# A two-layer hybrid attention block: mixer parts recorded in a common time, attention steps regrouped, early feed-forward chunks cut from six to four

## The chip, the cores and the metric

The kernel is one program on one NeuronCore of a Trainium2 chip. The metric is the device time of one execution in microseconds. Inputs lie in device memory when the time starts; the host only reorders weights. Engine names are those of the profile: PE (TensorE matmuls), PEld (its weight loads), DVE (VectorE), ACT (ScalarE), POOL (GpSimd), SP (SyncE, which issues the DMAs).

## The reference

One sequence of 512 tokens with 1024 features passes through two layers. Each layer has a first feed-forward block, a mixer and a second feed-forward block, with a layer norm after each (`ALPHA * x` is added first; the feed-forward outputs are halved). All values are 32-bit floats.

```python
D_MODEL, SEQ, DEPTH, D_FF = 1024, 512, 2, 2816
N_GROUPS, HEADS, HEAD_DIM, D_GROUP, Q_BLOCK = 4, 4, 64, 256, 128

def swiglu(x, w1, w3, w2):
    return (jax.nn.silu(x @ w1) * (x @ w3)) @ w2

def hybrid_mixer(x, w_in, ...):
    h = split_columns(x @ w_in)
    y_a = mla_mixer(...)              # latent attention, softmax
    y_b = nsa_mixer(...)              # compressed + selected + window attention, gated
    y_c = dsa_mixer(...)              # an indexer picks the top keys, then softmax attention
    y_d = stick_breaking_mixer(...)
    y = jnp.concatenate([y_a, y_b, y_c, y_d], -1).reshape(B, S, N_GROUPS, D_GROUP)
    y = rms_norm(y, group_norm_g.reshape(N_GROUPS, D_GROUP)).reshape(B, S, D_MIX)
    return y @ w_out

def masked_softmax(s, mask):
    s = jnp.where(mask, s, NEG_INF)
    e = jnp.where(mask, jnp.exp(s - jnp.max(s, -1, keepdims=True)), 0.0)
    return e / jnp.maximum(jnp.sum(e, -1, keepdims=True), 1e-30)
```

Each mixer group has four heads of width 64, and works through four blocks of 128 queries. In block b only the first (b + 1) * 128 keys count.

## The kernel before

**Numbers.** A 32-bit product of the large matrices is made of three passes: each factor is split in a rounded part (`hi`) and the rest (`lo`), and `mm3` issues hi*hi, hi*lo and lo*hi. A weight unit (`wunit`) is a DMA of 128 x 1024 values into a `raw` buffer, a rounding copy into `whi` and a DVE subtraction into `wlo`. The input x of each stage lies transposed in `xhi` and `xlo`; the residual stream lies in `z`.

**Feed-forward.** The hidden width is cut in 22 chunks of 128. A chunk has an up part (w1 and w3), and its down part (w2) follows when a group of chunks is there: for each of the four token blocks and each half of the output one PSUM tile collects the group, and DVE adds it to `z`. There are two kinds of up part. `up` is plain: 8 x 3 matmuls for each of w1 and w3, with 512 tokens, or 256 where half of the tokens are treated. `up_pair` takes both weights together over combinations of token halves and weight halves (a Strassen-like scheme): 7 products of 4 x 3 matmuls with 256 columns, after `token_sums` has formed the sums and differences of x on DVE. In layer 0 the first block takes its first two chunks plainly and all others by `up_pair`.

**The second feed-forward block in two halves.** `EARLY` chunks are taken for tokens 0 to 255 inside the mixer (`ffn_half(..., 0)`, called the filler) and for tokens 256 to 511 after it (`ffn_half(..., 1)`), both with plain `up`; `REST` chunks follow by `up_pair`.

**The mixer.** It consists of Python generators: `index_proj`, `sb_proj`, `mla_proj`, `nsa_proj`, `dsa_proj` project; `index_scores` and `choose` score keys and pick 128 of them by 16 steps of `max` and `match_replace` on DVE for each of three blocks (the tiles named `acc`); `sb_attend`, `mla_attend`, `nsa_attend`, `dsa_attend` are the groups. The three softmax groups go through `attend`: for each head scores into a PSUM tile `ps`, a maximum on DVE, an exponential on ACT that also sums, transposes on PE, a copy, and the product with the values into `po`. `group_out` then normalizes a group's block, multiplies it with `w_out` and adds to `z`; `dsa_attend` ends a block with its layer norm. `proj_rope` projects, copies out of PSUM (`evac`) and rotates (`roped`).

**What sets the order.** Every operation is recorded (so nearly all carry line 400, the call in `emit`; copies carry 388, scaled copies 396). `Plan.schedule` then plays the program with its own cost table and gives every engine the ready operation that was recorded first, if its buffers can be had; a buffer out of turn is given only while more than `reserve` of its kind are free. An operation for "scalar/vector" goes to whichever is free, except that DVE leaves it when ACT will be free within `BEHIND` ns. The recording order is thus the priority. It is written by `weave`, which steps a main generator and others at a rate, for instance `weave(mla_attend((1, 0, 3, 2)), (npj, 0.3), (chooser, 1.3))`, and `drain`.

Of the kernel before, what the change touches and what calls it, by code (L numbers as in the profile page):

```python
# [14 lines left out]
OP = mybir.AluOpType  # L15
# [11 lines left out]
EARLY = (3, 3)  # L27
REST = (6, 5, 5)
# [4 lines left out]
WA = 468  # L33
# [110 lines left out]
class Plan:  # L144
# [4 lines left out]
    BEHIND = 700  # L149
# [93 lines left out]
    def schedule(self):  # L243
# [42 lines left out]
        while left:  # L286
            progress = True
            while progress:
                progress = False
                for e in engines:  # L290
# [4 lines left out]
                    while h:  # L295
                        x = heapq.heappop(h)[2]
                        x.queued.discard(e)
                        if x.start is None and eligible(x):
                            if e == "vector" and "scalar" in x.costs and free_at["scalar"] < now + self.BEHIND:
# [177 lines left out]
def block_kernel(ctx, tc, ins, out, dbg=None):  # L477
# [13 lines left out]
    t_lo = pl.tag(sb, "wlo", 6, [1024], F32R, reserve=2)  # L491
# [7 lines left out]
    singles = {n: pl.tag(sb, n, 1, [w]) for n, w in (("mv", 4 * 256), ("acc23", 7 * P))}  # L499
# [345 lines left out]
    def roped(zs, spans):  # L845

        sw, o = tmp(), ht()
        rope = rope_now[0]
        for r0, rn, tb in spans:
# [10 lines left out]
    def proj_rope(w, spans, scale=None):  # L860
        return roped(evac(projT(w), tmp(), scale), spans)
# [11 lines left out]
    def attend(b, qk, v, mask, o, rs):  # L873

        n = (b + 1) * P
        sums = small(4)
        for h in range(4):
            s = psc()
            for i, (q, k) in enumerate(qk(h)):
                PE.matmul(s[:, :n], q, k, start=(i == 0), stop=False)  # L880
            if mask is None:
                PE.matmul(s[:, n - P:n], identb, maskd, start=False, stop=True)
            else:
                PE.matmul(s[:, :n], identb, mask, start=False, stop=True)
            m = small(1)
            V.tensor_reduce(m, s[:, :n], axis=AX, op=OP.max, negate=True)
            e = tmp()
            A.activation(e[:, :n], s[:, :n], AF.Exp, bias=m, accum_out=sums[:, h:h + 1])
            pt = transposed(None, e, n)
            et = tmp()  # L890
            AV.tensor_copy(et[:, :n], pt[:, :n])
            for j in range(b + 1):
                PE.matmul(o[:, h * 64:(h + 1) * 64], et[:, j * P:(j + 1) * P], v(h, j), start=(j == 0), stop=(j == b))
            yield
        V.tensor_scalar(rs, sums, 1e-30, None, op0=OP.max)
        V.reciprocal(rs, rs)

    def heads(t):
        return t.split(4)

# [6 lines left out]
    def group_out(b, y, gcol, wo):  # L907
# [4 lines left out]
        r = rsqrt(ss, 1, 1e-6)  # L912
        pt = ptr()
        for c in range(2):
            PE.transpose(pt[:, c * P:(c + 1) * P], y[:, c * P:(c + 1) * P], ident)
        yh = pl.buf(t_yh, [2, P], F32R)
        yl = pl.buf(t_yl, [2, P], F32R)
        for c in range(2):
            cs = slice(c * P, (c + 1) * P)
            AV.scaled(yh[:, c, :], pt[:, cs], gcol[:, c:c + 1])  # L920
            V.scalar_tensor_tensor(yl[:, c, :], pt[:, cs], gcol[:, c:c + 1], yh[:, c, :].bitcast(F32),
                                   op0=OP.mult, op1=OP.subtract)
        for n in range(2):
            ns = slice(n * 512, (n + 1) * 512)
            p = pm()
            for c in range(2):
                mm3(p, (yh[:, c, :], yl[:, c, :]), (wo[c][0][:, ns], wo[c][1][:, ns]), c == 0, c == 1)
            V.scalar_tensor_tensor(z[:, b, ns], p, r, z[:, b, ns], op0=OP.mult, op1=OP.add)


    def weave(main, *others):

        due = [0.0] * len(others)
        for _ in main:
            for i, (gen, rate) in enumerate(others):
                due[i] += rate
                while due[i] >= 1:
                    due[i] -= 1
                    next(gen, None)
# [5 lines left out]
    def mixer(l, filler):  # L945
# [7 lines left out]
        def wout(g):  # L953
            return [wunit(wo[(2 * g + c) * P:(2 * g + c + 1) * P, :]) for c in range(2)]
# [36 lines left out]
        V_SLC, V_WIN, V_DSA, V_SB, V_G, V_IW = 0, 64, 128, 192, 448, 460  # L991
# [80 lines left out]
        def sb_attend(blocks):  # L1072
            w_sb = wout(3)
            for b in blocks:
# [26 lines left out]
                group_out(b, y, gc[:, 6:8], w_sb)  # L1101
# [5 lines left out]
        mv = single("mv", [NB, 256])  # L1107

        def mla_proj():
# [40 lines left out]
            for c in (2, 0, 1):  # L1150
# [3 lines left out]
                if c == 2:  # L1154
                    qr = roped(evac(p, tmp(), M_SCALE), FULL_I)
# [12 lines left out]
            for h in range(4):  # L1168
                move(mk[h][64:96, :], krT[0:32, :])
            for b in range(NB):  # L1170
                p = pm()
                PE.matmul(p[:, :256], ckT[:, b * P:(b + 1) * P], uk[:, 256:512], start=True, stop=True)
                AV.tensor_copy(mv[:, b, :], p[:, :256])
            yield

        def mla_attend(blocks):
            w_mla = wout(0)
            for b in blocks:
# [4 lines left out]
                                  lambda h, j: mv[:, j, h * 64:(h + 1) * 64], None, o, rs)  # L1183
                y = ytile()
                V.tensor_tensor(heads(y), heads(o[:, :256]), bc(rs), op=OP.mult)
                dump(f"y_a{l}_{b}", y)
                group_out(b, y, gc[:, 0:2], w_mla)
# [98 lines left out]
        def nsa_attend(blocks):  # L1286
            w_nsa = wout(1)
            kslc, kwin, ec = nk
            for b in blocks:
# [7 lines left out]
                for g, (kk, v0) in enumerate(((kslc, V_SLC), (kwin, V_WIN))):  # L1297
# [20 lines left out]
        def dsa_attend(blocks, gb):  # L1318
            w_dsa = wout(2)
            for b in blocks:  # L1320
# [5 lines left out]
                                  lambda h, j: vt[:, j, V_DSA:V_DSA + 64], None if b == 0 else bias[b][:, :n], o, rs)  # L1326
                y = ytile()
                V.tensor_tensor(heads(y), heads(o[:, :256]), bc(rs), op=OP.mult)
                dump(f"y_c{l}_{b}", y)
                group_out(b, y, gc[:, 4:6], w_dsa)  # L1330
# [9 lines left out]
        drain(index_proj())  # L1340
        drain(sb_proj())
        isc = index_scores((3, 2, 1))
        mp = mla_proj()
        weave(sb_attend(range(NB)), (isc, 1.5), (mp, 0.3), (chooser, 0))
        drain(isc)
        drain(mp)
        pl.ln = False
        npj, dpj = nsa_proj(), dsa_proj()
        weave(mla_attend((1, 0, 3, 2)), (npj, 0.3), (chooser, 1.3))
        drain(npj)  # L1350
        weave(nsa_attend((0, 1)), (dpj, 0.15), (chooser, 0.8))
        drain(dpj)
        gb = single("rg", [4, 512])
        gb = ln_load(ins["ln2_g"][l], ins["ln2_b"][l], [[gb[:, 2 * i + n, :] for n in range(2)] for i in range(2)])
        while bias[1].buf.dtype != BF16:
            next(chooser)
        weave(dsa_attend((1, 0), gb), (chooser, 0.5))
        weave(nsa_attend((3, 2)), (filler, 0.15), (chooser, 0.7))
        drain(chooser)
        weave(dsa_attend((3, 2), gb), (filler, 0.3))  # L1360
        drain(filler)

    for l in range(DEPTH):
        ffn(ins["f1w13"][l], ins["f1w2"][l], ins["ln1_g"][l], ins["ln1_b"][l], 0, PARTS, (0, 1) if l else None, False)
        mixer(l, ffn_half(ins["f2w13"][l], ins["f2w2"][l], 0))
        weave(ffn_half(ins["f2w13"][l], ins["f2w2"][l], 1))
# [58 lines left out]
def layout(inputs):  # L1425
# [12 lines left out]
    for n, cols in (("wA", COLS_A), ("wB", COLS_B)):  # L1438
        o[n] = w_in[:, :, cols].reshape(L, 4, 2, P, len(cols)).transpose(0, 1, 3, 2, 4)
# [39 lines left out]
```

## Time and profile before

| | us |
|---|---|
| runs shown | 2109.18, 2110.53, 2104.78 (median 2109.18) |
| profiled execution | 2103.86, span 2102.0 |
| PE, PEld busy | 2035.8, 1805.0 |
| DVE, ACT busy | 1722.0, 1014.7 |
| mean granted TensorE clock | 0.983 |

The program alternates long feed-forward stretches with two mixers. By the times of the first and last operations of its parts, the mixer of layer 0 fills roughly 427 to 730 us of the span, that of layer 1 the same 303 us from 1471 to 1774. The busy rows of a window tell for each engine how many us of it were busy and, in brackets, how many instructions; matmuls are pipelined and their ends modelled, so the distance of their starts says more than their durations. The granted clock of a window is 1.00 where the PE ran at full speed throughout.

### The profile page before, as it was taken

What the parts mean: (1) busy time and instruction counts of PE and PEld (TensorE: products, weight loads), DVE (VectorE), ACT (ScalarE), POOL (GpSimd) and SP (SyncE); (2) the same over time, 40 slices, a digit from 0 to 9 for tenths busy, and PEclk for the clock granted to TensorE, in tenths of its full rate; (3) what the DMA queues carried; (4) which work ended last, traced back from release to release, by engine and by line L of the source; (5) the groups of instructions that cost most, each with busy time, mean ns of one, the idle gap of its engine ahead of it and who ended that gap; (6) DMA issues with size and microseconds to landing.
All of it is one profiled execution on the core that took longest, in us unless ns stands there. A gap on an engine that the chain in (4) does not pass through costs nothing.

```text
span 2102.0 us, 33862 instructions
## 1 busy us (share of the span) xinstructions
PE 2035.8 (97%) x13150; PEld 1805.0 (86%) x13154; DVE 1722.0 (82%) x3096; ACT 1014.7 (48%) x1891; POOL 74.4 (4%) x92
## 2 busy tenths in 40 slices
PE   7999999999999999999999999999999999999998
PEld 6998998876788899899888989987767788998997
DVE  8786979669997869697996968786699968796978
ACT  5343533478465545353342524434875655453531
POOL 0000001000000100000000000010000001000000
PEclk9999999999999999999999999999999999999999
DMA  5322413412121353232322333243121214433422
GB/s 192 116 98 93 141 71 137 124 57 81 61 76 46 103 188 111 100 122 90 121 71 101 111 99 132 77 149 119 45 71 61 81 51 140 156 112 104 137 75 101
DMA packets 66241, 216.64 MB, mean 103 GB/s; under 512 B 8736, under 2 KB 11296, under 8 KB 65824
## 3 DMA queue, kind: packets, MB, share of 16 engines
q1 hardware_dynamic: 66080, 214.48, 29.9%
q8 instruction: 103, 1.69, 0.3%
q14 instruction: 58, 0.48, 0.1%
HBM read 207.63 MB, written 2.10 MB: 100 GB/s over the span
## 4 chain that ended last, share of the span: by engine, by line
PE 67%; DVE 21%; ACT 4%; issue 4%; DMA 3%; POOL 0%; SPq 0%; DVEq 0%; ACTq 0%; POOLq 0%
PE pm L400 45%; PE ps L400 9%; PE po L400 8%; PE pt L400 6%; DVE wlo L400 5%; DVE ln L400 4%; DVE acc L400 2%; DVE T L400 2%; DVE s L400 2%; DMA raw<-in_f1w_dram 1%; DVE z L400 1%; DVE e L400 1%; ACT e L400 1%; DVE mv L400 1%; ACT whi L388 1%
## 5 line engine op out<-in xcount | busy, mean ns | idle before, releaser
L388 ACT ACTIVATE whi<-raw 128x1024 fp32r<-128x1024 f32 (+3 forms) x366 | 348.9, 963 | 359.8 <-PE pm L400 291.0
L400 PE MATMUL pm<-whi,T 128*128 128x512 f32 x1408 | 446.4, 395 | 7.4 <-DVE z L400 3.5
L400 DVE TENSOR_TENSOR wlo<-raw,whi 128x1024 fp32r<-128x1024 f32 (+3 forms) x295 | 358.1, 1218 | 59.7 <-ACT whi L388 57.6
L400 PEld LDWEIGHTS pm<-whi,T 128*128 128x128 f32 x1408 | 263.4, 188 | 73.4 <-ACT T L388 6.5
L400 PE MATMUL pm<-xhi,whi 128*128 128x256 f32 (+1 forms) x976 | 307.3, 315 | 7.0 <-ACT xhi L388 6.1
L400 PE MATMUL pm<-xhi,wlo 128*128 128x256 f32 (+1 forms) x976 | 304.0, 312 | 1.4 <-DVE wlo L400 1.3
L400 PE MATMUL pm<-xlo,whi 128*128 128x256 f32 (+1 forms) x976 | 304.8, 312 | 0.2 <-DVE xlo L400 0.2
L400 PE MATMUL pm<-wlo,T 128*128 128x512 f32 x704 | 274.4, 393 | 0.3 <-DVE wlo L400 0.3
L400 DVE SCALAR_TENSOR_TENSOR z<-pm,z 128x512 f32<-128x512 f32 x144 | 98.6, 688 | 175.4 <-PE pm L400 175.3
L388 ACT ACTIVATE whi<-ln 128x1024 fp32r<-128x1024 f32 x144 | 150.4, 1058 | 145.9 <-DVE z L400 86.0
L400 PEld LDWEIGHTS pm<-xhi,whi 128*128 128x128 f32 x976 | 185.3, 190 | 19.1 <-ACT xhi L388 6.4
L400 PEld LDWEIGHTS pm<-xhi,wlo 128*128 128x128 f32 x976 | 185.0, 190 | 11.7 <-DVE wlo L400 2.2
L400 PEld LDWEIGHTS pm<-xlo,whi 128*128 128x128 f32 x976 | 184.8, 189 | 10.2 <-DVE xlo L400 1.3
L400 DVE TENSOR_TENSOR wlo<-ln,whi 128x1024 fp32r<-128x1024 f32 x144 | 174.4, 1218 | 4.4 <-ACT whi L388 4.4
L400 PE MATMUL ps<-xhi,wlo 128*128 128x256 f32 x576 | 160.8, 279 | 0.0
L400 PE MATMUL ps<-xlo,whi 128*128 128x256 f32 x576 | 160.7, 279 | 0.0
L400 PE MATMUL ps<-xhi,whi 128*128 128x256 f32 x576 | 160.7, 279 | 0.0
L400 PEld LDWEIGHTS pm<-wlo,T 128*128 128x128 f32 x704 | 132.2, 188 | 29.2 <-DVE wlo L400 2.1
L400 PE MATMUL ps<-T,T 128*128 128x512 f32 (+11 forms) x400 | 129.9, 403 | 4.7 <-ACT e L391 2.2
L400 PE MATMUL pm<-T,whi 128*128 128x256 f32 x864 | 117.0, 283 | 10.8 <-ACT whi L388 7.0
L400 PEld LDWEIGHTS pm<-T,whi 128*128 128x128 f32 x864 | 108.8, 190 | 12.0 <-ACT whi L388 7.4
L388 ACT ACTIVATE T<-e 128x512 fp32r<-128x512 f32 (+2 forms) x116 | 65.3, 563 | 105.1 <-DVE e L400 79.1
(188 smaller groups left out, 4345.6 us busy)
## 6 DMA issues: line engine op xcount, KB each, us to landing
raw<-in_f2w_dram SPq DMA_DIRECT2D x168, 512.0 KB, 3.6
raw<-in_f1w_dram SPq DMA_DIRECT2D x131, 512.0 KB, 3.6
raw<-in_wT_dram SPq DMA_DIRECT2D x26, 512.0 KB, 3.3
raw<-in_w_out_dram SPq DMA_DIRECT2D x24, 512.0 KB, 3.2
raw<-in_wA_dram SPq DMA_DIRECT2D x8, 468.0 KB, 4.8
raw<-in_wB_dram SPq DMA_DIRECT2D x8, 416.0 KB, 3.3
e<-T SPq DMA_DIRECT2D x64, 48.0 KB, 1.9
ln<-in_x_dram SPq DMA_DIRECT2D x4, 512.0 KB, 4.3
```

Of the source, the lines that this page charges most:

```text
L388: self.nc.scalar.activation(*args, AF.Copy)
L400: getattr(getattr(self.nc, o.eng), o.fn)(*args, **kw)
```

## The change

- **Feed-forward groups.** `EARLY` goes from (3, 3) to (4,), `REST` from (6, 5, 5) to (6, 6, 6). In the very first block, chunks 2 and 3 are taken plainly as well, so `token_sums` is recorded two chunks later.
- **Recording order.** `weave` goes. `play` gives every part a span in a common time (`SPANS`: start, end, steps), always steps the part whose next step is earliest, and first completes what the part needs.
- **Attention steps.** In blocks 0 and 1 four and two heads share one `ps` tile, with one maximum and one copy. The sum of the exponentials comes from a column of ones beside the values (`vt`, `mv`: 65 columns a head) instead of from the exponential's accumulator, so it is read out of `po` after the last product.
- **Group output.** The gain is multiplied into the `w_out` units as they are split, and the group's transposed block is copied and subtracted in one piece each.
- **Rotation.** `roped` reads the projection out of PSUM, with the scale inside its multiplications; the copy goes (not in the compressed part, whose copy is also used unrotated).
- **Planner.** `BEHIND` goes from 700 to 400, the reserve of `wlo` from 2 to 3.

```diff
-EARLY = (3, 3)
-REST = (6, 5, 5)
+EARLY = (4,)
+REST = (6, 6, 6)
+SPANS = {"ip": (0, 5, 6), "sp": (6.7, 9.3, 5), "is": (2.8, 17.4, 25), "sa": (12.3, 30, 21), "mp": (12, 32, 10),
+         "ma": (33, 55, 21), "np": (23.4, 53.5, 8), "na": (53.2, 72.8, 21), "nb": (83.3, 92.3, 21),
+         "dp": (56.1, 68, 3), "ln": (68.8, 69.8, 1), "da": (73.5, 75, 13), "db": (76.4, 99.2, 13),
+         "ch": (25.6, 103.2, 52), "ff": (82.7, 114.9, 13)}
-WA = 468
+WA = 472
-    BEHIND = 700
-    t_lo = pl.tag(sb, "wlo", 6, [1024], F32R, reserve=2)
+    t_lo = pl.tag(sb, "wlo", 6, [1024], F32R, reserve=3)
...
+    def wunit(src, n=1024, cuts=1, gain=None):
...
+            if gain is None:
+                parts(hi[:, c], lo[:, c], raw[:, c])
+            else:
+                AV.scaled(hi[:, c], rv, gain)
+                V.scalar_tensor_tensor(lo[:, c], rv, gain, f32(hi[:, c]), op0=OP.mult, op1=OP.subtract)
...
-                if xs is None and (m + c > 1 or not first):
+                if xs is None and (m + c > 3 or not first):
                     xs = token_sums()
...
+            times(o[rs, :], zs[rs, :], rope[rs, tb, :])
             V.stream_shuffle(sw[rs, :], zs[rs, :], SWAP)
-            V.tensor_tensor(o[rs, :], zs[rs, :], rope[rs, tb, :], op=OP.mult)
-            V.tensor_tensor(sw[rs, :], sw[rs, :], rope[rs, tb + 1, :], op=OP.mult)
+            times(sw[rs, :], sw[rs, :], rope[rs, tb + 1, :])
...
-        return roped(evac(projT(w), tmp(), scale), spans)
+        return roped(projT(w), spans, scale)
...
+        g = max(1, 512 // n) if b < 2 else 1
+        for h0 in range(0, 4, g):
             s = psc()
+            m = small(g)
...
+            V.tensor_reduce(m, s[:, :g * n].split(g) if g > 1 else s[:, :n], axis=AX, op=OP.max, negate=True)
...
-            A.activation(e[:, :n], s[:, :n], AF.Exp, bias=m, accum_out=sums[:, h:h + 1])
+                A.activation(e[:, c], s[:, c], AF.Exp, bias=m[:, h - h0:h - h0 + 1])
...
+                    PE.matmul(o[:, h * 65:(h + 1) * 65], et[:, c:c + P], v(h, j), start=(j == 0), stop=(j == b))
...
-        V.tensor_scalar(rs, sums, 1e-30, None, op0=OP.max)
+        V.tensor_scalar(rs, o[:, 64:260:65], 1e-30, None, op0=OP.max)
...
+        AV.tensor_copy(yh, pv)
+        V.tensor_tensor(yl, pv, f32(yh), op=OP.subtract)
...
+    def play(gens, spans, needs):
+        made = dict.fromkeys(gens, 0)
+        over = set()
+        def step(k):
+            if not made[k]:
+                for other, n in needs.get(k, ()):
+                    while made[other] < n and other not in over:
+                        step(other)
+            made[k] += 1
+            for _ in gens[k]:
+                return
+            over.add(k)
+            pl.ln = pl.ln and k != "sa"
+        while len(over) < len(gens):
+            step(min((k for k in gens if k not in over),
+                     key=lambda k: spans[k][0] + (spans[k][1] - spans[k][0]) * made[k] / spans[k][2]))
...
+        play(parts_, SPANS, {
+            "is": (("ip", 99),), "sa": (("sp", 99),), "ma": (("mp", 99),), "na": (("np", 99),), "nb": (("np", 99),),
+            "da": (("na", 99), ("ln", 99), ("dp", 99), ("ch", 17), ("ip", 99)), "db": (("nb", 99), ("ch", 99), ("da", 99)),
+            "ch": (("is", 99),), "ln": (("dp", 99), ("np", 99), ("mp", 99), ("ip", 99)), "ff": (("da", 99),)})
```

The keys are the parts: ip index_proj, sp sb_proj, is index_scores, sa sb_attend, mp/ma mla, np nsa_proj, na and nb nsa_attend of blocks 0, 1 and 3, 2, dp dsa_proj, ln the loads of the norm's gains, da and db dsa_attend of blocks 1, 0 and 3, 2, ch the choosing, ff the filler.

More of the change, by code (lines that the diff above doesn't have):

```diff
@@ L298, in schedule @@
                         if x.start is None and eligible(x):
-                            if e == "vector" and "scalar" in x.costs and free_at["scalar"] < now + self.BEHIND:
+                            if e == "vector" and "scalar" in x.costs and free_at["scalar"] < now + 400:
                                 later.append(x)
@@ L498, in block_kernel @@
     t_s = pl.tag(sb, "s", 28, [16], reserve=7)
-    singles = {n: pl.tag(sb, n, 1, [w]) for n, w in (("mv", 4 * 256), ("acc23", 7 * P))}
+    singles = {n: pl.tag(sb, n, 1, [w]) for n, w in (("mv", 4 * 260), ("acc23", 7 * P))}
     def single(name, shape, dt=F32):
@@ L843, in evac, with roped, times @@
         return t
-    def roped(zs, spans):
+    def roped(zs, spans, scale=None):
         sw, o = tmp(), ht()
         rope = rope_now[0]
+        def times(out, x, t):
+            if scale is None:
+                V.tensor_tensor(out, x, t, op=OP.mult)
+            else:
+                V.scalar_tensor_tensor(out, x, scale, t, op0=OP.mult, op1=OP.mult)
         for r0, rn, tb in spans:
             rs = slice(r0, r0 + rn)
+            times(o[rs, :], zs[rs, :], rope[rs, tb, :])
             V.stream_shuffle(sw[rs, :], zs[rs, :], SWAP)
-            V.tensor_tensor(o[rs, :], zs[rs, :], rope[rs, tb, :], op=OP.mult)
-            V.tensor_tensor(sw[rs, :], sw[rs, :], rope[rs, tb + 1, :], op=OP.mult)
+            times(sw[rs, :], sw[rs, :], rope[rs, tb + 1, :])
             V.tensor_tensor(o[rs, :], o[rs, :], sw[rs, :], op=OP.add)
@@ L875, in attend @@
         n = (b + 1) * P
-        sums = small(4)
-        for h in range(4):
+        g = max(1, 512 // n) if b < 2 else 1
+        for h0 in range(0, 4, g):
             s = psc()
[L879 to L886, printed above, removed]
+            m = small(g)
+            for h in range(h0, h0 + g):
+                sh = s[:, (h - h0) * n:(h - h0 + 1) * n]
+                for i, (q, k) in enumerate(qk(h)):
+                    PE.matmul(sh, q, k, start=(i == 0), stop=False)
+                if mask is None:
+                    PE.matmul(sh[:, n - P:], identb, maskd, start=False, stop=True)
+                else:
+                    PE.matmul(sh, identb, mask, start=False, stop=True)
+            V.tensor_reduce(m, s[:, :g * n].split(g) if g > 1 else s[:, :n], axis=AX, op=OP.max, negate=True)
             e = tmp()
-            A.activation(e[:, :n], s[:, :n], AF.Exp, bias=m, accum_out=sums[:, h:h + 1])
-            pt = transposed(None, e, n)
+            for h in range(h0, h0 + g):
+                c = slice((h - h0) * n, (h - h0 + 1) * n)
+                A.activation(e[:, c], s[:, c], AF.Exp, bias=m[:, h - h0:h - h0 + 1])
+            pt = transposed(None, e, g * n)
             et = tmp()
[L891 to L894, printed above, removed]
-        V.tensor_scalar(rs, sums, 1e-30, None, op0=OP.max)
+            AV.tensor_copy(et[:, :g * n], pt[:, :g * n])
+            for h in range(h0, h0 + g):
+                for j in range(b + 1):
+                    c = ((h - h0) * (b + 1) + j) * P
+                    PE.matmul(o[:, h * 65:(h + 1) * 65], et[:, c:c + P], v(h, j), start=(j == 0), stop=(j == b))
+            for _ in range(g):
+                yield
+        V.tensor_scalar(rs, o[:, 64:260:65], 1e-30, None, op0=OP.max)
         V.reciprocal(rs, rs)
@@ L899, in heads, with values @@
         return t.split(4)
+    def values(o):
+        return o[:, :260].split(4)[:, :, :64]
     def bc(t):
@@ L905, in ytile, with group_r @@
         return pl.buf(t_y, [256])
[L907 removed]
+    def group_r(y):
         scr = pl.buf(t_y, [256])
@@ L911, in group_out, with normed @@
         A.activation(scr, y, AF.Square, scale=1.0 / 16.0, accum_out=ss)
-        r = rsqrt(ss, 1, 1e-6)
-        pt = ptr()
[L914 to L922, printed above, removed]
+        return rsqrt(ss, 1, 1e-6)
+    def normed(y):
+        r = group_r(y)
+        yn = ytile()
+        AV.scaled(yn, y, r)
+        return yn
+    def group_out(b, ys, wo, r=None):
+        m = 2 * len(ys)
+        pt = ptr()
+        for c in reversed(range(m)):
+            PE.transpose(pt[:, c * P:(c + 1) * P], ys[c // 2][:, c % 2 * P:(c % 2 + 1) * P], ident)
+        yh, yl = pl.buf(t_yh, [m, P], F32R), pl.buf(t_yl, [m, P], F32R)
+        pv = pt[:, :m * P].split(m)
+        AV.tensor_copy(yh, pv)
+        V.tensor_tensor(yl, pv, f32(yh), op=OP.subtract)
         for n in range(2):
@@ L925, in group_out @@
             p = pm()
[L926 to L939, printed above, removed]
+            for c in range(m):
+                mm3(p, (yh[:, c, :], yl[:, c, :]), (wo[c][0][:, ns], wo[c][1][:, ns]), c == 0, c == m - 1)
+            V.scalar_tensor_tensor(z[:, b, ns], p, 1.0 if r is None else r, z[:, b, ns], op0=OP.mult, op1=OP.add)
+    def play(gens, spans, needs):
[14 more added lines that the diff above has]
+                     key=lambda k: spans[k][0] + (spans[k][1] - spans[k][0]) * made[k] / spans[k][2]))
     def drain(gen):
@@ L953, in wout @@
         def wout(g):
-            return [wunit(wo[(2 * g + c) * P:(2 * g + c + 1) * P, :]) for c in range(2)]
+            return [wunit(wo[(2 * g + c) * P:(2 * g + c + 1) * P, :], gain=gc[:, 2 * g + c:2 * g + c + 1]) for c in range(2)]
         def half(h):
@@ L1106, in mixer @@
         M_SCALE = float(96.0 ** -0.5)
-        mv = single("mv", [NB, 256])
+        mv = single("mv", [NB, 4, 65])
         def mla_proj():
@@ L1325, in dsa_attend @@
                 yield from attend(b, lambda h: [(dq[h][:, ts], k[:, :n]) for k in dk],
-                                  lambda h, j: vt[:, j, V_DSA:V_DSA + 64], None if b == 0 else bias[b][:, :n], o, rs)
+                                  lambda h, j: vt[:, j, V_DSA:V_DSA + 65], None if b == 0 else bias[b][:, :n], o, rs)
                 y = ytile()
-                V.tensor_tensor(heads(y), heads(o[:, :256]), bc(rs), op=OP.mult)
+                V.tensor_tensor(heads(y), values(o), bc(rs), op=OP.mult)
                 dump(f"y_c{l}_{b}", y)
-                group_out(b, y, gc[:, 4:6], w_dsa)
+                group_out(b, [y], w_dsa, group_r(y))
                 yield
@@ L1338, in chain, with ln2_load @@
                 yield from g
[L1340 to L1361, printed above, removed]
+        gb = []
+        def ln2_load():
+            t = single("rg", [4, 512])
+            gb.extend(ln_load(ins["ln2_g"][l], ins["ln2_b"][l], [[t[:, 2 * i + n, :] for n in range(2)] for i in range(2)]))
+            yield
+        parts_ = {
+            "ip": index_proj(), "sp": sb_proj(), "is": index_scores((3, 2, 1)), "sa": sb_attend(range(NB)),
+            "mp": mla_proj(), "ma": mla_attend((1, 0, 3, 2)), "np": nsa_proj(), "na": nsa_attend((0, 1)),
+            "nb": nsa_attend((3, 2)), "dp": dsa_proj(), "ln": ln2_load(), "da": dsa_attend((1, 0), gb),
+            "db": dsa_attend((3, 2), gb), "ch": chooser, "ff": filler}
+        play(parts_, SPANS, {
[3 rows of a table added]
     for l in range(DEPTH):
@@ L1438, in layout @@
     for n, cols in (("wA", COLS_A), ("wB", COLS_B)):
-        o[n] = w_in[:, :, cols].reshape(L, 4, 2, P, len(cols)).transpose(0, 1, 3, 2, 4)
+        w = w_in[:, :, cols]
+        if n == "wA":
+            w = np.insert(w, (64, 128, 192, 468), 0, axis=2)
+        o[n] = w.reshape(L, 4, 2, P, -1).transpose(0, 1, 3, 2, 4)
     o["w_out"] = g["w_out"]
```

26 lines of the change are left out of this document (13 added, 13 removed).

## The prediction

> **What bounds the kernel now.** I read the page first, then windows over the stages, then groups of instructions by shape, and last the starts of single matmuls. On the page PE looks like the bound.
>
> ```profile
> span 2102.0 us, 33862 instructions
> PE 2035.8 (97%) x13150; PEld 1805.0 (86%) x13154; DVE 1722.0 (82%) x3096; ACT 1014.7 (48%) x1891; POOL 74.4 (4%) x92
> ```
>
> The windows (columns: PE, PEld, DVE, ACT, POOL busy, granted clock, DMA) say where that holds:
>
> ```profile
> 32.28:50.00 17.72, 10.37 (x61) 9.73 (x60) 17.68 (x23) 8.53 (x12) 0.00 (x0) 0.71 0.32 119
> 50.00:82.50 32.50, 32.50 (x279) 32.50 (x278) 31.47 (x44) 19.45 (x28) 0.00 (x0) 1.00 0.41 141
> 82.50:427.00 344.50, 343.23 (x2175) 309.23 (x2174) 262.81 (x386) 135.57 (x196) 8.14 (x8) 1.00 0.33 109
> 427.00:480.00 53.00, 49.91 (x254) 39.48 (x254) 36.02 (x98) 45.49 (x141) 4.81 (x6) 0.97 0.15 51
> 480.00:650.00 170.00, 159.89 (x881) 125.77 (x881) 165.38 (x462) 105.55 (x268) 8.37 (x13) 0.94 0.20 69
> 650.00:700.00 50.00, 50.00 (x373) 46.43 (x376) 32.02 (x75) 32.12 (x75) 2.70 (x4) 0.97 0.21 75
> 700.00:730.00 30.00, 26.28 (x159) 21.92 (x157) 26.93 (x59) 12.57 (x26) 4.54 (x5) 1.00 0.26 88
> ...
> 1524.00:1694.00 170.00, 160.08 (x890) 125.90 (x889) 165.99 (x463) 105.96 (x269) 9.03 (x14) 0.95 0.21 69
> ```
>
> The feed-forward stretch (82.5 to 427) is PE's: weight loads fill 90% of it at clock 1.00, DVE 76%. The mixer has three stages. A (427 to 480) is ACT's, 45.5 of 53. B (480 to 650) is DVE's, 165.4 of 170 (97%), while weight loads fill only 74%. C (650 to 730) begins with 50 us in which PE is full, by the filler, and ends in a tail. Layer 1 shows B again, 166.0 of 170. And early on, from 32 to 50 us, DVE is full and PE is not.
>
> [...] By the 97% of PE alone the change would be worth its matmuls, some 3 us; by the 74% in B there is room, and the agreement of B's low clock (0.94) with the second reading is why I follow it.
>
> **The change, part by part: the start.** The first rows are PE's in order of time (start, duration, what, idle before and who ended it), the next two are pieces of the chain that ended last (start, duration, what):
>
> ```profile
> 28.78 0.40 PE L400 MATMUL pm<-xhi,whi 128*128 128x512 f32 x1
> ...
> 32.05 0.40 PE L400 MATMUL pm<-xhi,wlo 128*128 128x512 f32 x1
> ...
> 40.09 1.01 PE L400 MATMUL pm<-T,whi 128*128 128x256 f32 x2 [4.93 <-ACT whi L388]
> 43.53 1.01 PE L400 MATMUL pm<-T,whi 128*128 128x256 f32 x3 [2.43 <-DVE whi L400]
> ```
>
> ```profile
> 54.43 2.84 PE po L400 x24
> ...
> 79.69 35.93 PE pm L400 x168
> ```
>
> Two groups of DVE (behind the bar: busy us, mean ns of one; idle before):
>
> ```profile
> L400 DVE TENSOR_TENSOR wlo<-raw,whi 128x1024 fp32r<-128x1024 f32 x277 | 338.5, 1226 | 54.4 <-ACT whi L388 52.7 <-PE pm L400 0.8
> ...
> L400 DVE TENSOR_TENSOR T<-e,T 128x512 fp32r<-128x512 f32 x74 | 50.8, 687 | 8.1 <-ACT T L388 7.7
> ```
>
> From 28.78 to 32.05 fourteen 512-wide matmuls start: 0.2336 us each. 24 of 256 take 2.84: 0.118 each. So a plain chunk is 48 x 0.2336 = 11.2 us, a pair chunk 84 x 0.118 = 9.9. Chunks 2 to 5, all pairs now, go from 32.28 to 82.5 (24 products of the 168 pieces after 79.69 are still theirs): 50.2 us for 336 x 0.118 = 39.6, because PE stands for 4.93 and 2.43 us while DVE forms the token sums, and then runs slowly (clock 0.71). After: 96 x 0.2336 + 168 x 0.118 = 42.2 us, **-8.0**. The cover: the sums and the first pair's weights, ready at 43.5 now, come behind the plain chunks' DVE work, four `wlo` (1.226) and four passes of 512 (0.687), 7.7 us, so at 51.2; the plain chunks hold PE until 32.3 + 22.4 = 54.7. If that cover fails, the stall only moves: bound +2.6 (the dearer chunks).
>
> **The early group.** A chunk's up part is 48 x 0.118 = 5.66 us a half; its down part 12 x 0.2336 = 2.8 a half. Two chunks less: the filler loses 2 x 8.46 = 16.9 us of PE, the second half the same, and the pair stretch gains 2 x (9.9 + 5.6) = 31.0. Outside the mixers, where PE is full, that is 31.0 - 16.9 = **+14.1 a layer**. DVE, at 76% there, covers its part. Inside, 16.9 us of PE go from C.
>
> **DVE and ACT in the mixer.** More groups of one shape each:
>
> ```profile
> L400 DVE TENSOR_REDUCE s<-ps 128x1 f32<-128x128 f32 x32 | 8.5, 281 | 0.0
> ...
> L400 DVE TENSOR_REDUCE s<-ps 128x1 f32<-128x256 f32 x32 | 13.2, 414 | 0.2 <-PE ps L400 0.2
> ...
> L400 DVE TENSOR_REDUCE s<-ps 128x1 f32<-128x512 f32 x32 | 21.4, 678 | 2.7 <-PE ps L400 2.7
> ...
> L388 ACT ACTIVATE e<-pt 128x128 f32<-128x128 f32 x40 | 10.3, 276 | 10.7 <-PE pt L400 8.6 <-PE ps L400 1.9
> ...
> L388 ACT ACTIVATE e<-pt 128x256 f32<-128x256 f32 x40 | 15.1, 382 | 12.6 <-PE pt L400 12.1
> ...
> L388 ACT ACTIVATE e<-pt 128x512 f32<-128x512 f32 x39 | 22.9, 594 | 17.2 <-PE pt L400 12.7 <-PE ps L400 4.2
> ...
> L400 ACT ACTIVATION_READ_ACCUMULATOR e<-ps,s 128x1 f32 x128 | 25.3, 198 | 0.0
> ...
> L396 ACT ACTIVATE yh<-pt,gc 128x128 fp32r<-128x128 f32 x64 | 23.5, 368 | 10.3 <-DVE yl L400 7.6 <-PE pt L400 1.7
> ...
> L400 DVE SCALAR_TENSOR_TENSOR yl<-pt,gc,yh 128x128 fp32r<-128x128 f32 x64 | 22.0, 344 | 2.3 <-ACT yh L396 2.1
> ...
> L400 DVE TENSOR_TENSOR e<-e,pm 128x256 f32<-128x256 f32 x28 | 11.7, 418 | 10.9 <-PE pm L400 10.8
> ...
> L400 DVE SCALAR_TENSOR_TENSOR z<-pm,z 128x512 f32<-128x512 f32 x144 | 98.6, 688 | 175.4 <-PE pm L400 175.3
> ...
> L400 DVE SCALAR_TENSOR_TENSOR z<-pm,s,z 128x512 f32<-128x512 f32 x64 | 46.9, 745 | 14.3 <-PE pm L400 14.2
> ...
> L388 ACT ACTIVATE e<-pm 128x512 f32<-128x512 f32 x10 | 5.9, 591 | 5.6 <-PE pm L400 5.5
> ...
> L400 DVE TENSOR_TENSOR T<-e,rg 128x512 f32<-128x512 f32 x16 | 10.9, 680 | 0.0
> ...
> L400 DVE TENSOR_TENSOR xlo<-pt,xhi 128x512 fp32r<-128x512 f32 x40 | 26.3, 684 | 6.3 <-ACT xhi L388 6.0
> ...
> L400 DVE MAX8 s<-acc 128x8 f32<-128x384 f32 x32 | 17.7, 552 | 0.1
> ...
> L400 DVE MATCH_REPLACE8 acc<-s,acc 128x384 f32<-128x384 f32 x32 | 17.4, 543 | 0.0
> ...
> L400 PE MATMUL po<-vt,e 128*128 128x64 f32 x640 | 91.4, 280 | 4.5 <-ACT e L388 3.7
> ```
>
> All a layer, in DVE us. Maxima: four calls of `attend` meet each block; block 0 saves 4 x 0.281 - 0.678 = 0.446 a call, block 1 4 x 0.414 - 2 x 0.678 = 0.300: 3.0. Group output: two of 0.344 become one of 0.418: 0.270 x 16 = 4.3. The gain: eight `wlo` with a column scalar, which costs 745 - 688 = 57 ns: -0.5. The filler's two chunks: six `wlo` (7.4), six passes of 256 (2.5), four additions to `z` (2.7): 12.6. New memsets of ones, at most 0.281 each by the 128-wide maximum, at least nothing: -0.5 for five. DVE loses **18.9 us** in the mixer. ACT loses 64 accumulator reads (12.7), copies (4 x (4 x 0.276 - 0.594) + 4 x (4 x 0.382 - 2 x 0.594) = 3.4), nine evacuations (5.3) and, in group output, 16 x (2 x 0.368 - 0.382) = 5.7; but ACT binds in A alone, where only four group outputs fall.
>
> What costs: the sums now come from `po` after the last product, so two small operations lie behind it, about 0.3 us a call; B's chooser and C's filler cover all but the last block. A 65th column: 64 columns already take 280 ns where 512 take 0.2336 between starts, so I take nothing; bound 1/64 of 91.4, 1.4. A rotation holds its `pm` tile for two DVE passes instead of one ACT copy; nothing, if DVE is prompt, else a projection's 5.6 us (24 x 0.2336) is waited for in part. Whether DVE pays for PSUM: 684 ns from `pt`, 680 from `e`: 0.004 us x 20 passes, nothing. `BEHIND` moves copies to DVE whenever ACT is 0.4 us late, which helps in A and hurts in B; no row prices it: I take zero, between a gain of A's excess of ACT over DVE (9.5) and the same loss in B.
>
> [...]
>
> **The order.** The rows of the choosing and scoring tiles alone show where they stand:
>
> ```profile
> 427.00:480.00 53.00, 11.23 (x20) 0.00 (x0) 0.97 0.15 51
> 480.00:650.00 170.00, 56.66 (x152) 0.00 (x0) 0.94 0.20 69
> 650.00:730.00 80.00, 0.00 (x0) 0.00 (x0) 0.98 0.23 80
> ```
>
> 56.7 us of B's 165.4 are this chain; A has 17.0 us of idle DVE, C 21.0. The change records scoring ahead of the stick-breaking group and choosing from 25.6 on, before the latent attention, so part goes to A; and `db` first records all of `nb`, so the last 17 choosing steps (16 x 1.095 = 17.5 us) fall behind `nb`, partly in C. I credit a third of each, 5.7 and 5.8, since A's scores need projections first and DVE's gaps are short. Block 3 of `db` needs none of these steps, so they queue with it, not before it.
>
> **The sum.** A stays 53. B: 3.0 + 2.2 (eight group outputs) - 0.4 + 11.5 = 16.3 less of DVE at its 97%: 170 - 17 = 153. C: 80 - 16.9 = 63, where DVE has 59.0 - 12.6 - 1.1 + 5.8 = 51; 66, as the tail is a chain. The mixer goes from 303 to **272 us**. Against the profiled 2103.9: -8.0 + 2 x (-31 + 14.1) = -41.8, so 2062. That execution lies 5 us under the median of the runs shown; I say **2065**. The mixer's break-even against the 2104 is at 303 - 14.1 + 4.0 = 293 us.
>
> **Rivals.** *The cover is gone (slower).* The mixer's wall is set by its chains and not by the filler: the 16.9 us leave holes, and reappear outside at 14.1. Place: after 650, where choosing, `db` and the norms queue on DVE with 33.8 us of filler in place of 50.7. For it: at 700 to 730 PE already waits, though the filler is there. Against: 650 to 700 is full of PE. With 303 us: 2104 - 8 + 28 = 2124. It decides from a mixer above 293.
> *The mixer packs (much faster).* DVE's 260.4 - 18.9 = 241.5 us at B's 97% throughout: 249. 2104 - 8 + 2 x (-54 + 14.1) = 2016. For it: each engine has idle time where another is full. Against: chains at both ends.
> *The change does little.* If PE is the bound throughout, only its matmuls count, -2.8 a layer and +2.6 at the start: 2101. If B's DVE does not shrink, the mixer gives back only what the filler took (289) and the start's stall moves, it is 2104 + 2.6 = 2106.
>
> **Chances.** Forecast, a mixer of 262 to 284 (2042 to 2086): 0.52. Packed, under 262: 0.13. Between, 284 to 292 (2086 to 2103): 0.15. No change (within 0.3%, about what a measurement here can tell): 0.08. Slower: 0.12. Faster is 0.52 + 0.13 + 0.15 = 0.80. The range takes in all but about half of the packed case and most of the slower one: 2028 to 2108; the forecast's own is 2042 to 2086.
>
> **What would show it.** Right: no gap over 1 us on PE between 32 and 60 us; idle DVE under 10 us in A's 53; 10 us or more of `acc` work before stage B beyond today's 11.2; no accumulator reads for exponentials; DVE busy over 85% across a mixer of about 272 us; the pair stretches 31 us longer a layer. Wrong: gaps of PE behind DVE at the end of the mixer, or projections that wait for a `pm` tile.

## The result, and the profile after

| | before | after |
|---|---|---|
| median, us | 2108.01 (2104.78 to 2110.53) | 2055.05 (2050.27 to 2057.89) |
| ratio | | 0.9749, 95% interval 0.9729 to 0.9769 |
| profiled execution, us | 2103.86 | 2050.27 |
| mean granted clock | 0.983 | 0.995 |

2065 was forecast, 2055 came: 53 us less, in a range of 2028 to 2108. The total came out near; two of its terms did not, and they had opposite signs. Head of the page after:

```profile
span 2048.5 us, 33197 instructions
PE 2008.7 (98%) x13030; PEld 1779.4 (87%) x13034; DVE 1714.3 (84%) x3050; ACT 957.2 (47%) x1625; POOL 75.5 (4%) x92
```

PE's busy time falls by 27 us, its share rises; DVE has almost the work that it had, ACT 57 us less. To see where the time went, I cut both executions at the last normalization statistics (`BATCH_NORM_STATS2`) of each block, which does not depend on how parts are ordered. This mixer is 51 us longer than the 303 us given ahead of the prediction: its first projections, at 366 to 427 us of the span before, belong to it, and were counted there to the feed-forward stretch.

| us | first block, layer 0 | mixer 0 | to its end | first block, layer 1 | mixer 1 | to its end |
|---|---|---|---|---|---|---|
| before | 365.6 | 354.1 | 336.1 | 353.6 | 353.9 | 331.0 |
| after | 358.4 | 338.0 | 332.5 | 352.5 | 329.1 | 330.4 |
| change | -7.2 | -16.1 | -3.6 | -1.1 | -24.8 | -0.6 |

"To its end" holds the rest of the filler, the second half and the pair stretch. The windows after (PE, PEld, DVE, ACT, POOL busy, granted clock, DMA): first the start, then the mixer of layer 0 and what follows it, then layer 1's mixer. Each mixer is cut at the last scan of the stick-breaking group, into a first and a second phase.

```profile
32.28:50.00 17.72, 17.72 (x78) 14.37 (x77) 17.69 (x20) 8.22 (x11) 0.00 (x0) 1.00 0.20 70
...
358.40:502.50 144.10, 142.81 (x687) 110.74 (x686) 119.61 (x269) 95.95 (x223) 7.82 (x10) 1.00 0.28 89
502.50:696.40 193.90, 186.24 (x1207) 158.03 (x1208) 174.28 (x449) 98.68 (x193) 13.33 (x19) 0.97 0.21 71
696.40:1028.90 332.50, 331.48 (x2313) 306.17 (x2313) 279.62 (x401) 142.28 (x199) 7.60 (x8) 1.00 0.33 113
1381.40:1525.40 144.00, 142.78 (x687) 110.79 (x686) 119.66 (x269) 96.16 (x223) 7.75 (x10) 1.00 0.28 89
1525.40:1710.40 185.00, 179.21 (x1197) 153.12 (x1198) 170.87 (x446) 99.22 (x194) 14.00 (x19) 1.00 0.22 73
```

The same cuts before:

```profile
365.60:502.40 136.80, 131.20 (x617) 101.03 (x616) 98.02 (x205) 93.05 (x225) 8.44 (x10) 0.99 0.26 82
502.40:719.70 217.30, 206.14 (x1280) 175.16 (x1281) 192.96 (x531) 126.91 (x318) 13.08 (x19) 0.95 0.20 71
719.70:1055.80 336.10, 333.35 (x2323) 307.14 (x2324) 277.53 (x396) 143.14 (x200) 6.52 (x7) 1.00 0.35 121
1409.50:1546.40 136.90, 131.30 (x617) 101.04 (x616) 98.03 (x205) 93.21 (x225) 8.44 (x10) 0.99 0.26 84
1546.40:1763.40 217.00, 207.14 (x1286) 175.06 (x1287) 194.97 (x532) 125.68 (x316) 13.10 (x19) 0.95 0.21 72
```

The first phase became 7 us longer, but holds 22 us more of DVE and 70 more matmuls; PE is busy in 142.8 of 144.1 us at full clock. The second lost 23 us (32 in layer 1) with 19 us of DVE and 28 of ACT. DVE's sum over mixer 0 did not fall at all (291.0 to 293.9; in mixer 1 it fell by 2.5): the work was packed, not shed. The rows of the choosing and scoring tiles say what was brought forward, before and after:

```profile
365.60:502.40 136.80, 20.49 (x40) 0.00 (x0) 0.99 0.26 82
502.40:719.70 217.30, 48.14 (x132) 0.00 (x0) 0.95 0.20 71
```

```profile
358.40:502.50 144.10, 32.31 (x79) 0.00 (x0) 1.00 0.28 89
502.50:696.40 193.90, 36.21 (x92) 0.00 (x0) 0.97 0.21 71
```

At the start, the waits of 4.93 and 2.43 us are gone from PE: 17.72 of 17.72 us busy, clock 1.00 in place of 0.71. The lighter steps, as groups of one shape after (copies and scaled copies carry other lines here, and all else 403 in place of 400):

```profile
L403 DVE SCALAR_TENSOR_TENSOR wlo<-raw,gc,whi 128x1024 fp32r<-128x1024 f32 x24 | 30.7, 1278 | 1.0 <-ACT whi L399 0.9
...
L403 ACT ACTIVATE e<-ps,s 128x512 f32<-128x512 f32 x32 | 21.8, 688 | 17.4 <-DVE s L403 14.4 <-DVE rc L403 3.0
...
L403 DVE TENSOR_TENSOR yl<-pt,yh 128x256 fp32r<-128x256 f32 x32 | 13.3, 415 | 0.4
...
L403 DVE STREAM_SHUFFLE e<-pm 128x512 f32<-128x512 f32 x16 | 11.8, 735 | 0.0
...
L403 DVE SCALAR_TENSOR_TENSOR T<-pm,rg 128x512 f32<-128x512 f32 x10 | 6.8, 685 | 0.0
...
L403 DVE TENSOR_SCALAR s<-po 128x4 f32<-128x4 f32 x32 | 4.9, 153 | 4.8 <-PE po L403 4.7
```

### The profile page after: what moved, and what is told of

It reads as the page before. It is cut to its first block, busy times and chain, and to the rows that moved or that the text cites. A ratio compares the mean times of both kernels' runs of the same rounds, so it can differ in the third digit from the quotient of the medians.

```text
span 2048.5 us, 33197 instructions
## 1 busy us (share of the span) xinstructions
PE 2008.7 (98%) x13030; PEld 1779.4 (87%) x13034; DVE 1714.3 (84%) x3050; ACT 957.2 (47%) x1625; POOL 75.5 (4%) x92
## 4 chain that ended last, share of the span: by engine, by line
PE 71%; DVE 20%; DMA 4%; issue 3%; ACT 2%; POOL 0%; SPq 0%; DVEq 0%; ACTq 0%
PE pm L403 44%; PE ps L403 11%; PE po L403 10%; PE pt L403 6%; DVE wlo L403 5%; DVE ln L403 3%; DVE T L403 2%; DVE s L403 2%; DVE acc L403 2%; DMA raw<-in_f1w_dram 2%; DVE e L403 2%; DMA raw<-in_f2w_dram 1%; DVE z L403 1%; DVE mv L403 1%; ACT whi L391 1%
## 5 line engine op out<-in xcount | busy, mean ns | idle before, releaser
L391 ACT ACTIVATE whi<-raw 128x1024 fp32r<-128x1024 f32 (+3 forms) x327 | 308.3, 951 | 389.2 <-PE pm L403 314.8
L403 DVE TENSOR_TENSOR wlo<-raw,whi 128x1024 fp32r<-128x1024 f32 (+3 forms) x257 | 311.0, 1212 | 42.2 <-ACT whi L391 40.1
L403 PE MATMUL pm<-xhi,whi 128*128 128x256 f32 (+1 forms) x888 | 285.3, 322 | 7.2 <-ACT xhi L391 6.2
L403 PE MATMUL pm<-xlo,whi 128*128 128x256 f32 (+1 forms) x888 | 284.1, 320 | 0.2 <-DVE xlo L403 0.2
L403 PE MATMUL pm<-xhi,wlo 128*128 128x256 f32 (+1 forms) x888 | 283.4, 319 | 1.0 <-DVE s L403 0.9
L403 PEld LDWEIGHTS pm<-xhi,whi 128*128 128x128 f32 x888 | 168.1, 189 | 19.7 <-ACT xhi L391 6.6
L403 PEld LDWEIGHTS pm<-xhi,wlo 128*128 128x128 f32 x888 | 168.3, 190 | 12.8 <-DVE wlo L403 1.9
L403 PEld LDWEIGHTS pm<-xlo,whi 128*128 128x128 f32 x888 | 168.3, 189 | 12.4 <-DVE xlo L403 0.9
L403 PE MATMUL ps<-T,T 128*128 128x384 f32 (+12 forms) x400 | 122.2, 393 | 5.0 <-ACT e L403 3.2
L403 POOL TENSOR_TENSOR s<-s,epow 128x1 f32<-128x1 f32 (+1 forms) x64 | 47.3, 740 | 1861.8 <-DVE s L403 1841.0
```

The costliest lines, as they stand in the source:

```text
L391: self.nc.scalar.activation(*args, AF.Copy)
L403: getattr(getattr(self.nc, o.eng), o.fn)(*args, **kw)
```

## The experiments

All times are medians; a ratio is to the kernel before, run beside it. The changed kernel's own ratio is 0.9749, so a difference of 0.001 is 2.1 us. `u_` marks the changed kernel with one thing undone, `x_` and e2 the changed kernel with one thing taken further. A replay is what the planner makes of a recording: a small change early in it can alter the order of operations later, in parts whose code is the same. No run undoes the group output, the rotation or the reserve of `wlo` alone.

**How far a single replay can be read: null1 and null2.**

```diff
-                            t = int(now // self.TICK)
+                            t = int((now + 1138) // self.TICK)   # 2275 in null2; its two neighbours alike
```

> A control: the changed kernel, its operations and their recording order untouched; only the phase of the 3.4 us windows in which the planner guesses PE's clock is shifted by a third of a window, so that the planner breaks near-ties otherwise. If single undone parts can be read to a few us: 2055 within 4. If any replay of the planner moves a mixer by 7 us, as layer 1's moved when only layer 0's first block was changed: 2045 to 2070.

> The same control with two thirds of a window: the same two expectations, a second draw.

2058.68 (0.9767, 0.9752 to 0.9781) and 2056.34 (0.9757, 0.9732 to 0.9781). Mixer 0 took 341.4 and 342.4 us against 338.0, mixer 1 the same 329 in both. By these two draws, differences of the whole under some 4 us say nothing. For a single mixer the limit is wider, as u_start below shows. The first phase of a mixer hardly scatters: 144.1 us in mixer 0 in both controls, as in the changed kernel.

**The start: u_start.**

```diff
-                if xs is None and (m + c > 3 or not first):
+                if xs is None and (m + c > 1 or not first):
```

> The changed kernel with the token sums of the very first block formed two chunks earlier again (chunks 2 and 3 by pairs). Both theories: the stall between 35 and 44 us returns with the slow clock behind it, +7 to +8: 2062 to 2063. If the stall was paid elsewhere: 2052 (the plain chunks' dearer matmuls saved).

2069.60 (0.9809, 0.9785 to 0.9833), +13 by the ratios. PE's waits between 30 and 85 us, where the changed kernel shows none:

```profile
PE pm L403 <- ACT whi L391: 5.5, 1, 5.5
PE pm L403 <- DVE whi L403: 2.4, 1, 2.4
```

The first block is 368.3 us long against 358.4: the stall is the cause there. What ends both waits in the trace are weights (`whi`) of the first pair chunk, one of them made on DVE behind the token sums. Mixer 1 took 336.4 us against 329.1, though nothing in it was changed; 20 more up matmuls of the filler (176 against 156) stand ahead of its last norm there, which is 2.4 us of it. So a replay alone can move one mixer by 7 us, and a difference of that size in one mixer says little by itself.

**The early group: u_early.**

```diff
-EARLY = (4,)
-REST = (6, 6, 6)
+EARLY = (3, 3)
+REST = (6, 5, 5)
...
-         ... "ff": (82.7, 114.9, 13)}
+         ... "ff": (82.7, 114.9, 21)}
```

> The changed kernel with the early groups (3, 3) and the rest (6, 5, 5) put back (the filler's 21 steps over the same span). Surplus theory: the filler was more than the mixer's holes could take, so two chunks more change only the matmuls, 2 x 2.8 us, and show after the mixer: 2060, the last norm of each mixer within 3 us of where the changed kernel has it. The prediction's term: 16.9 us come back inside each mixer and 14.1 leave outside, also 2060, but with the last norm 16 us later relative to the first block's end. If DVE's 12.6 us a layer count: 2070 or more.

2071.44 (0.9823, 0.9802 to 0.9845), +16. Only the third expectation, DVE's 12.6 us a layer, has this number, but not its work: DVE has 297.0 us in mixer 0 (119.6 in the first phase and 177.4 in the second) against 293.9, so 3.1 more.

```profile
503.90:707.30 203.40, 195.65 (x1230) 164.87 (x1229) 177.38 (x452) 100.51 (x196) 13.33 (x19) 0.95 0.21 68
```

By the sign that was set for the other two, the place of the last norm, neither is right: it comes 9.5 and 7.8 us later in the mixers, not under 3 and not 16. What can be counted is how many matmuls of the filler stand ahead of the mixer's last norm (a third of the 256-wide up matmuls in that stretch; before, after, u_early):

```profile
L400 PE MATMUL pm<-xhi,whi 128*128 128x256 f32 x56 | 16.9, 302 | 0.5 <-DVE z L400 0.3 <-ACT whi L388 0.2
```

```profile
L403 PE MATMUL pm<-xhi,whi 128*128 128x256 f32 x56 | 16.4, 296 | 0.0
```

```profile
L403 PE MATMUL pm<-xhi,whi 128*128 128x256 f32 x56 | 16.3, 295 | 0.0
```

56 in all three, so some 168 of 288 (before, u_early) or of 192 (after) up matmuls; in layer 1 of the changed kernel 156. Before, the rest of the six chunks ran behind the norm. So between before and after the prediction's 16.9 us did not leave the mixer. (168 is no limit of what the mixer can take: u_order below has all 192 ahead of the norm.) The stretch behind it took 333.9 us in u_early and 332.5 in the changed kernel, the mixers 347.5 and 336.9 against 338.0 and 329.1. In u_early 19 down matmuls also stand ahead of the norm, 4.4 us in each layer. The other 5 and 3 us of the mixers are not settled; a replay can move a mixer by as much.

**The order undone: u_order; and alone: d_order.** u_order puts `weave` and its old calls into the changed kernel, d_order puts `play` and the spans into the kernel before.

```diff
-        play(parts_, SPANS, {...})
+        drain(index_proj())
+        drain(sb_proj())
+        weave(sb_attend(range(NB)), (isc, 1.5), (mp, 0.3), (chooser, 0))
+        ...
```

> The changed kernel with the old recording order (weave and its rates) put back; all else as changed. Order theory: the mixers' gain comes from scoring and choosing being recorded ahead of the stick-breaking group, so that DVE is full some 40 us earlier; without it some 30 of the two mixers' 38 us go: 2080 to 2092 against 2055. Lighter-steps theory: the gain comes from the DVE and ACT work that is gone, the order is worth at most 10: 2055 to 2065.

> The kernel before with the new recording order alone (play and the spans, the filler's 21 steps over its span); attention steps, rotation, group output, groups (3, 3), start and planner constants as before. Order theory: most of the mixers' 38 us, 2075 to 2090 against 2109. Lighter-steps theory: 2100 or slower, since the spans only pay with lighter steps.

u_order: 2081.84 (0.9869, 0.9846 to 0.9892), +25, as the order theory said; in mixer 0 the second phase is long again, 210.1 us with 191.7 of DVE. d_order: 2099.02 (0.9962, 0.9943 to 0.9982), only 8 us faster than before, against that theory and at the number of the other (2100). The phases of d_order:

```profile
367.10:518.50 151.40, 144.75 (x686) 112.05 (x685) 126.27 (x292) 102.94 (x241) 7.84 (x10) 0.99 0.28 88
518.50:716.50 198.00, 187.29 (x1230) 159.17 (x1230) 168.47 (x449) 114.96 (x299) 13.51 (x19) 0.98 0.20 67
```

The second phase has the gain, 198 in place of 217, but the first pays most of it back: 151 in place of 137, with 103 us of ACT in place of 93. The order brings work into the stretch in which ACT is loaded too.

**Who carries ACT's copies: u_behind.**

```diff
-                            if e == "vector" and "scalar" in x.costs and free_at["scalar"] < now + 400:
+                            if e == "vector" and "scalar" in x.costs and free_at["scalar"] < now + 700:
```

> The changed kernel with BEHIND back at 700, so that DVE leaves a copy whenever ACT will be free within 0.7 us. If DVE's taking of copies is what lets the new order pay in the first phase (144 us here, 151.5 in the kernel with the new order alone): the first phase returns toward 150 and the time to 2065 to 2075. If it only moves some 7 us of copies a layer from one full engine to the other: 2050 to 2062.

2072.00 (0.9825, 0.9802 to 0.9847), +16. Its phases:

```profile
358.60:511.30 152.70, 147.40 (x689) 112.70 (x688) 125.89 (x289) 99.89 (x231) 7.82 (x10) 0.98 0.28 87
511.30:706.20 194.90, 186.43 (x1216) 158.36 (x1216) 163.32 (x413) 103.54 (x202) 13.71 (x19) 0.97 0.21 69
```

The first phase is back at 152.7, as long as in the kernel with the order alone, although all lighter steps are in. In mixer 1 it is 152.6. The seven other runs that change nothing of this phase have 144.0 or 144.1 in mixer 0, so this is no scatter: the planner's constant, one line, is what keeps the price of the new order in the first phase at 7 us. (The constant changes which copies the planner gives away and with that the order; which of the two counts is not told apart.) Between d_order and u_behind, both at 700, lie all the lighter steps, the early group and the reserve of `wlo`; their mixers differ by 1.8 and 6.3 us only, while u_attend below, at 400, moves the mixers by 12.4 and 14.9. So the gains of the parts do not add up.

**Early scoring and choosing alone: u_late; still earlier: x_ch.**

```diff
-         "is": (2.8, 17.4, 25), ... "ch": (25.6, 103.2, 52)
+         "is": (12.3, 30, 25), ... "ch": (33, 103.2, 52)       # u_late
+         "is": (2.8, 17.4, 25), ... "ch": (17.4, 103.2, 52)    # x_ch
```

> The changed kernel with two spans moved: scoring recorded beside the stick-breaking group (12.3 to 30 in place of 2.8 to 17.4) and choosing from 33 in place of 25.6; nothing else. Order theory in its narrow form (early scoring and choosing fill DVE while ACT binds): 15 to 25 us slower, 2070 to 2080, with DVE idle again before the stick-breaking ends. If the order matters by other parts (projections, the forced run of nsa before dsa): within the control's scatter of 2055.

> The changed kernel with choosing recorded from 17.4 in place of 25.6, so that more of its steps rank ahead of the stick-breaking group's later heads. If still more DVE work can be brought forward: first phase up by less than second phase falls, 2045 to 2052. If the first phase is full (DVE 120 of 144, ACT 96): a wash, 2052 to 2062.

u_late: 2104.49 (0.9982, 0.9964 to 1.0001), +49: two spans undo nearly the whole change. Its phases:

```profile
359.20:520.60 161.40, 152.19 (x679) 115.26 (x677) 110.72 (x225) 91.20 (x209) 9.01 (x10) 0.94 0.26 83
520.60:723.60 203.00, 189.56 (x1220) 160.39 (x1220) 190.97 (x509) 98.95 (x195) 14.00 (x19) 0.97 0.20 66
```

DVE is idle for 51 us of the first phase and then has 191 in the second. It is twice as bad as expected. In this order scoring ends at 164 us of mixer 0, behind the stick-breaking, where the old order ended it at 125 and the new one at 85, and choosing can't begin before; that this is why it is so bad is argued, and the two spans were not moved singly. x_ch: 2065.76 (0.9798, 0.9779 to 0.9818), +10, slower than expected: the first phase grew by 1.8 us and the second did not shrink (195.8, and 193.0 in layer 1). The span found in the change is not bettered by more of the same.

**The old attention step: u_attend.** `attend` as before, 64 columns, no ones.

```diff
...
+            A.activation(e[:, :n], s[:, :n], AF.Exp, bias=m, accum_out=sums[:, h:h + 1])
...
```

> The changed kernel with the old attention step (one head a tile, sums by the exponential's accumulator, 64 columns). Order theory: its 3.0 us of DVE and 16 us of ACT a layer lie mostly beside a full DVE: 3 to 8 us in all, 2058 to 2063. Lighter-steps theory: ACT's part counts too, 20 us or more: 2075.

2078.51 (0.9855, 0.9836 to 0.9874), +22: the lighter-steps theory's number. The first phase is untouched (144.1), the second takes it all:

```profile
503.60:709.90 206.30, 192.86 (x1202) 164.13 (x1201) 182.18 (x478) 104.32 (x268) 13.12 (x19) 0.93 0.20 65
```

8 us more of DVE there, not 3.0: beside the 20 maxima (3.0) seven copies `e<-pt` went to DVE (3.6), and the bounds of the sums take 1.0 more. ACT has its 64 accumulator reads again (12.5). Whether the shared tiles or the column of ones makes the difference is not told apart.

**Less choosing: x_half.**

```diff
-         ... "ch": (25.6, 103.2, 52), ...
+         ... "ch": (25.6, 91.3, 44), ...
...
-                for i in range(16):
+                for i in range(8 if b == 2 else 16):
```

> The changed kernel with half of the choosing for block 2 left out (8 of 16 steps of max and match_replace, so 64 keys are taken there in place of 128; its span is cut in proportion): 8 x 1.095 = 8.8 us of DVE a layer less, nothing else. If the mixer's second phase (from the last scan of the stick-breaking to the last norm) lasts as long as its DVE work and some 20 us: 7 to 9 us a layer, 2037 to 2041. If PE, the chains or the filler set it: within the control's scatter, 2051 to 2061.

2052.97 (0.9734, 0.9713 to 0.9754): no change beyond the control.

```profile
503.40:696.70 193.30, 186.34 (x1211) 159.08 (x1212) 167.69 (x427) 100.54 (x195) 13.20 (x19) 0.97 0.22 71
```

6.6 us of DVE are gone from the second phase, and it lasts 193.3 in place of 193.9 (186.7 in place of 185.0 in layer 1). So DVE, at 90%, is not the bound there by its sum. Block 2 is the last that is chosen for: these steps were free, which says nothing of those that others wait for.

**Too little cover: e2.**

```diff
-EARLY = (4,)
-REST = (6, 6, 6)
+EARLY = (2,)
+REST = (5, 5, 5, 5)
...
-         ... "ff": (82.7, 114.9, 13)}
+         ... "ff": (82.7, 114.9, 9)}
```

> The changed kernel with two early chunks in place of four (the rest in four groups of five, which adds eight additions to z a layer): 2 x 2.8 us of matmuls less, and a filler of 96 up matmuls and 24 down, 16.9 us, where the changed kernel plays 156 to 166 up matmuls before its last norm. Cover theory (the prediction's slower rival, now below the surplus): holes at the end of the mixer and before the second half, 2060 to 2075. If the filler's size does not matter even here: 2049.

2073.12 (0.9829, 0.9807 to 0.9851), +17 with 5.6 us less of matmuls. The mixers did not grow (337.9 and 326.3); the stretches behind them did, 343.3 and 342.9 against 332.5 and 330.4. PE's one long wait between 690 and 790 us:

```profile
PE pt L403 <- DVE ln L403: 8.1, 1, 8.1
```

The last layer norm runs with nothing beside it; the changed kernel's surplus of filler, 26 up and 48 down matmuls behind its norm, covers it. In layer 1 this wait is 5.4 us. The two waits are 13.5 of the 23 us by which the stretches grew; the rest is not traced to a cause.

## Why the prediction was right, and where it was not

**The start** was sized right: -8.0 forecast, -7.2 measured, the cover held (the first pair product starts at 54.45 us, 54.7 was said).

**The early group** is the term that failed: "inside, 16.9 us of PE go from C" and "+14.1 a layer" outside. Neither happened: outside went -3.6 and -0.6. I had taken the filler to be inside the mixer because 650 to 700 us was full of it; I did not count how many of its matmuls stood ahead of the last norm. 120 of the 288 and nearly all its down parts (all but one matmul in layer 0, seven in layer 1) stood behind it, and these are what the change cut. With them, the rise of the pair stretch and the fall of filler and second half cancel outside, as the matmul count says (2.8 a layer). The two wrong terms, -16.9 in the mixer and +14.1 outside, come from one wrong place and nearly cancel in the sum, which is why it stood. What u_early adds is open in part: put back into the changed kernel, the two chunks cost 9.5 and 7.8 us in the mixers, of which 4.4 are matmuls.

**The mixer**, 31 us less forecast, gave 16 and 25, so it went from the prediction's 303 to 287 and 278, not to 272. Without the filler's term the forecast had 14. "A stays 53" failed too: the first phase, which holds A, grew by 7.3 and 7.1 us. **DVE's 18.9 us** were mis-sized: +2.9 and -2.5 measured. The filler's 12.6 stayed; the gain is on 12 units a layer, not eight (nsa and dsa load theirs twice; the row shows 24 at 1278 ns, 52 more than 1226); and under `BEHIND` 400 DVE took copies. ACT lost 25.3 and 23.5 in the mixers; 27.1 was said. That the mixers came near what the forecast has without the filler is luck in part: DVE's work, which was to fall, did not, and more of it than was credited went to the first phase.

**The order**: of the scoring and choosing I credited 5.7 us to the first stage; between the cuts it was 11.8 (20.5 to 32.3), and DVE as a whole 22. That the order counts is shown by u_late and u_order; that the second phase follows DVE's sum, as I had it for stage B (170 us = 165.4 of work at 97%), is refuted by x_half for the changed kernel, whose DVE is full to 97% as well from 502 to 632 us; the kernel before was not tried. u_attend shows that the attention steps do count. The distinction that fits both is work on the chain against work beside it, but no run here isolates that chain.

**BEHIND** was given zero, as it might gain in A what it loses in B. By u_behind it is worth 16 us in the changed kernel.

**The small costs** were rightly nothing: a shuffle out of PSUM takes 735 ns (737 out of SBUF before), a rotation's multiplication 685 (680). So in these two pairs of rows the pass that reads PSUM takes 2 ns less and 5 ns more; the prediction's two rows had 4 more (684 and 680). The shuffle's row before:

```profile
L400 DVE STREAM_SHUFFLE e<-e 128x512 f32<-128x512 f32 x16 | 11.8, 737 | 0.1
```

**Rivals.** The cover did not go, because there was surplus; e2 shows the mechanism real below it, at another place than I said (after the last norm, not within choosing and `dsa`). The mixer did not pack to 249. Of the signs, PE shows no gap from 32 to 60 us, DVE is idle for 8.7 us of A's 53, the `acc` work ahead of stage B went from 12.0 to 23.8 us, the accumulator reads of the exponentials are gone, and DVE is busy over 85% of the mixer (87% and 88%); only the mixer's length was missed. The reading by which PE is the bound throughout would have given 2101 and is out. That the share of weight loads, 74% in B, tells PE's room was my assumption: no run tests it by itself.

The single undoings sum to more than 53 us (13, 16, 25, 16, 22), and the order alone gave 8: the parts are not shares of the gain. What sets the second phase now stays open.

## What to carry to other kernels

Before counting work as moved off a stage, count in the trace how much of it stands in that stage: of a filler in surplus, a cut first takes what ran behind the stage. The piece that covers the last norm must stay. Where two engines are full at different times, bring forward the long chain that only one needs, and see that the other engine of that stretch can give its copies away, as an order that pays in one phase may be paid back in the one before. And undo parts singly against a control that changes nothing but near-ties: here it scattered by 4 us in the whole, and one mixer moved by 7 in a run that changed nothing in it.

## What the runs showed of the hardware that was not expected

An exponential that also accumulates costs ACT no more in itself: 685 ns for 512 columns with (the row below, before), 688 without. The price is the separate read, 198 ns each, 128 of them before.

```profile
L400 ACT ACTIVATE e<-ps,s 128x512 f32<-128x512 f32 x32 | 21.9, 685 | 8.9 <-DVE s L400 8.7
```

In the second phase the granted clock went from 0.95 to 0.97 in mixer 0 and from 0.95 to 1.00 in mixer 1. The two play nearly the same operations (1207 and 1197 matmuls), in 193.9 and 185.0 us; no run tells whether the lower clock lengthens that phase or its waits lower the clock.
